# Gate rows of heads 1 to 3: from a product on TensorE to a broadcast load from DRAM

## The chip, the cores and the metric

The kernel runs on one core of a Trainium2 chip. The metric is the device time of one execution in microseconds (us), and the comparisons are between medians of several runs. A profile is one further execution, recorded by the hardware profiler. The engines are TensorE (PE in the rows; PEld is its weight load), VectorE (DVE), ScalarE (ACT), GpSimd (POOL) and SyncE (SP), which here only issues transfers.

## The reference

One encoder block works on 512 positions of 1024 channels. After an RMS norm, one projection makes the inputs of two branches. One branch is a Fourier mixing. The other is an mLSTM with 4 heads of 512 channels, run forward and backward. What matters here is the stabilised gate of the mLSTM. With `i` the input gate and `f` the log of the forget gate, per head and direction:

```python
bcum = jnp.cumsum(ft, axis=-1)
dmat = bcum[..., :, None] - bcum[..., None, :] + it[..., None, :]
m_t = jnp.maximum(bcum + m_st[..., None], jnp.max(dmat, axis=-1))
s_mat = jnp.einsum('bhtd,bhsd->bhts', qt, kt) * jnp.exp(dmat - m_t[..., None])
den = jnp.sum(s_mat, axis=-1) + inter * jnp.einsum('bhk,bhtk->bht', n_st, qt)
h_out = num / jnp.maximum(jnp.abs(den), jnp.exp(-m_t))[..., None]
```

The kernel computes the whole sequence at once instead of chunk by chunk. With `a = i - cumsum(f)` and `mx` the running maximum of `a` (starting at 0), the weight of source position s for target position t is `exp(a[s] - mx[t])`, and the stabiliser is `m = cumsum(f) + mx`. So each head and each direction needs two rows of 512 numbers in every partition: `mx` for the weights, and `m` for the lower bound `exp(-m)` of the denominator.

## The kernel before

The kernel is written with a tile framework. A planner orders each engine's instructions by simulated times, and it may move an instruction ahead of others that were written earlier. An instruction that is wrapped in `pin(...)` keeps its written order among the pinned ones. Tiles are taken by a tag. A new tile of the same tag takes the old one's place, and its first writer waits for the old one's last reader. PSUM is split into four banks of the tag `acc` and four of the tag `wk`.

The order of the work is: the projection of the mLSTM inputs and of a first gate (from the start to about 118 us), then four heads (to about 394 us, by the order of TensorE's products), then the mLSTM's output map, the Fourier branch and the merge. Products are made with float32 numbers split in two parts, a rounded part (ScalarE, `hi_of`, line 90) and the rest (VectorE, `lo_of`, line 93), and three products for one (`mm3`, lines 97 to 99).

Weights come in units of 128 x 1024 numbers. SyncE's queue loads a unit into one of three `raw` tiles (`fetch`, line 131; line 134 for halves), ScalarE and VectorE split it (`prepare`), and TensorE uses it. Each call of `unit()` splits one unit, hands out the one before it, and issues the fetch of the unit three further on. That fetch waits until VectorE has read the raw tile that it overwrites. The fetches are pinned. So are the copies of weight sums on SyncE's queue (line 159) and their accumulating counterparts on GpSimd's (line 163), which prepare sums for later stages (`sum_job`).

`gate_chain` (lines 420 to 457) runs once, in head 0. It makes, for all heads, a 64-row tile: row h is the forward direction of head h, row 32 + h the backward one. The last steps put the backward rows in natural order (lines 450 to 452). Then `mx` and `m` are split into a rounded part and a rest, in the tiles `mx_r` and `em_r` (lines 453 to 455), and `bsel`, a matrix of 8 selecting columns, is copied (line 456).

In each head:

- `decay` (line 512): for each direction TensorE multiplies a selecting column, repeated 128 times, with `mx_r` (line 516). That puts the head's row into all partitions of a PSUM bank. ScalarE makes the weights from it, eight exponentials (line 521) into the tiles `wf0` to `wf3`, and GpSimd cuts them at the diagonal (lines 525 and 528).
- The scores' products follow; VectorE multiplies them with the weights (lines 576 and 577) and sums them (lines 589 to 593).
- `o_unit` (lines 551 to 566, and 594 to 642) makes the output gate from four units. `o_gate` applies the sigmoid (line 572).
- The denominator: ScalarE writes a selecting tile `bw` (line 601), TensorE spreads the head's two rows of `em_r` with it (line 602, one product: the forward row in the upper 64 partitions and the backward row in the lower ones), and ScalarE takes `exp(-m)` (line 610). Line 608 sums the weighted scores. Line 612 takes their absolute value, line 613 the maximum of both, and line 614 the reciprocal.
- The weights are scaled and split (lines 622 to 628), values are made (line 636), the last output-gate unit follows (line 642), then the head's products, its norm (lines 652 to 658) and the transposes (line 668). Heads 1 to 3 also make their SiLU gate here, with `z_unit`.

Of the kernel before, what the change touches and what calls it, by code (L numbers as in the profile page):

```python
# [8 lines left out]
F32 = mybir.dt.float32  # L9
F32R = mybir.dt.float32r  # L10
AF = mybir.ActivationFunctionType
# [3 lines left out]
S = 512  # L15
D = 1024
P = 128
NH = 4
# [22 lines left out]
def hybrid_block(ctx: ExitStack, tc, xT, xn, first, units, blocks, vecs, gates, gbias, consts, dft, fnw, out):  # L41
    nc = tc.nc
    te, ve, se, gp = nc.tensor, nc.vector, nc.scalar, nc.gpsimd
# [17 lines left out]
    dram = ctx.enter_context(tc.tile_pool(name="sums", bufs=1, space=bass.MemoryType.DRAM))  # L61
# [3 lines left out]
    def tl(tag, shape, dtype=F32, bufs=1, pool=None, shift=0):  # L65
        count[0] += 1
        if pool is None:
            pool = "wide" if tag[:2] in ("sa", "sb") else "gw" if tag in ("gwh", "gwl") else "low" if tag in LOW else "high" if tag in HIGH else "work"


        n = math.prod(shape[1:])
        t = pools[pool][1].tile([shape[0], -(-(n + shift) // 64) * 64], dtype, tag=tag, name=f"{tag}_{count[0]}", bufs=bufs)
        t = t[:, shift : shift + n]
        if len(shape) == 2:
            return t
        names = "abcd"[: len(shape) - 1]
        return t.rearrange(f"p ({' '.join(names)}) -> p {' '.join(names)}", **dict(zip(names, shape[1:])))

    def bank(tag, cols=512, rows=P):
        count[0] += 1  # L80
        return ps.tile([rows, cols], F32, tag=tag, name=f"{tag}_{count[0]}", bufs=4)

    def t2k(dtype=F32, cols=S):
        return tl("t2k", [P, cols], dtype, bufs=3)

    def pin(ins, on=True):
        return tc.keep_in_program_order(ins) if on else ins
# [82 lines left out]
    def unit():  # L170
        i = state["split"]
        if state["at"] < len(JOBS) and i >= JOBS[state["at"]]:
            state["at"] += 1
            next_job()
        while len(items) < (4 if "gw" in pools else 2) and state["split"] < nplan:
            prepare()
        return items.pop(0)
# [39 lines left out]
    for n in range(4):  # L217
# [6 lines left out]
        for i in range(NU0):  # L224
            src, dst = slice(256 * i, 256 * i + 256), slice(256 * n, 256 * n + 256)
# [130 lines left out]
    def proj(hooks={}, pinned=False):  # L356
        wh, wl = unit()
        acc = bank("acc")
        for k in range(8):
            if k in hooks:  # L360
                hooks[k]()
            ks = slice(k * P, (k + 1) * P)
            mm3(acc, wh[:, ks], wl[:, ks], hv(x_hi, k), hv(x_lo, k), k == 0, k == 7, pinned or any(at <= k for at in hooks))
        return acc
# [19 lines left out]
    for n, (kind, i) in enumerate([("z", 0)] + [("x", i) for i in XO]):  # L384
# [6 lines left out]
        acc = early[n] if n < NU0 else proj(hooks, n == NU0 + 1)  # L391
# [24 lines left out]
    em_r = tl("em_r", [P, S], F32R)  # L416
    mx_r = tl("mx_r", [P, S], F32R)
    bsel = tl("bsel", [P, 8], F32R)

    def gate_chain():  # L420

        gb = tl("gb", [64, 2])
        pin(nc.sync.dma_start(gb, gbias))
        graw = t2k()
        se.activation(graw, gate_ps, AF.Copy)
        spare = [tl(t, [64, 2, S]) for t in ("so0", "so1")]
        s0, s1, s2, s3 = spare[0][:, 0, :], spare[0][:, 1, :], spare[1][:, 0, :], spare[1][:, 1, :]
        s4, s5 = tl("wf2", [64, S]), tl("wf3", [64, S])
        ig, z, e, u, w = s0, s1, s2, s3, s4
        for j, t in enumerate((ig, z)):  # L430
            sp = bank("acc", rows=64)
            te.matmul(sp, ident_c[:, C_SEL + 64 * j : C_SEL + 64 * j + 64], graw, start=True, stop=True)
            se.activation(t[0:32, :], sp[0:32, :], AF.Identity, bias=gb[0:32, j : j + 1])
            se.activation(t[32:64, ::-1], sp[32:64, :], AF.Identity, bias=gb[32:64, j : j + 1])
        se.activation(e, z, AF.Abs)
        se.activation(e, e, AF.Exp, scale=-1.0)
        ve.tensor_scalar(out=u, in0=e, scalar1=1.0, scalar2=None, op0=ALU.add)
        ve.scalar_tensor_tensor(out=w, in0=u, scalar=-1.0, in1=e, op0=ALU.add, op1=ALU.subtract)
        se.activation(u, u, AF.Ln)
        ve.scalar_tensor_tensor(out=w, in0=z, scalar=0.0, in1=w, op0=ALU.min, op1=ALU.add)  # L440
        ve.tensor_tensor(out=w, in0=w, in1=u, op=ALU.subtract)
        fc = e
        ve.tensor_tensor_scan(out=fc, data0=ones[0:64, 0:1].to_broadcast([64, S]), data1=w, initial=0.0,
                              op0=ALU.mult, op1=ALU.add)
        a, mx = u, z
        ve.tensor_tensor(out=a, in0=ig, in1=fc, op=ALU.subtract)
        ve.tensor_tensor_scan(out=mx, data0=a, data1=a, initial=0.0, op0=ALU.max, op1=ALU.max)
        ve.tensor_tensor(out=fc, in0=fc, in1=mx, op=ALU.add)
        an, mxn, mn = s5, s0, s4
        for dst, srct in ((an, a), (mxn, mx), (mn, fc)):  # L450
            ve.tensor_copy(dst[0:32, :], srct[0:32, :])
            ve.tensor_copy(dst[32:64, ::-1], srct[32:64, :])
        for dst, srct in ((mx_r, mxn), (em_r, mn)):
            se.activation(dst[0:64, :], srct, AF.Copy)
            ve.tensor_tensor(out=dst[64:128, :], in0=srct, in1=dst[0:64, :].bitcast(F32), op=ALU.subtract)
        pin(se.activation(bsel, ident_c[:, C_BSEL : C_BSEL + 8], AF.Copy))
        return an

    def gate_cols(an):
# [14 lines left out]
    for h in range(NH):  # L474
# [21 lines left out]
        for d in range(4):  # L496
            acc = bank("wk")
# [7 lines left out]
        if h == 0:  # L505
            rows = gate_chain()
# [5 lines left out]
        def decay():  # L512
            ws = [tl(f"wf{b}", [P, 640]) for b in range(4)]
            for dr in range(2):
                bc = bank("acc")
                te.matmul(bc, bsel[:, 4 * dr + h : 4 * dr + h + 1].to_broadcast([P, P]), mx_r, start=True, stop=True)
                for b in range(4):
                    n = (b + 1) * P
                    o, s = (slice(n, 640), slice(b * P, S)) if dr == 0 else (slice(0, n), slice(0, n))
                    r = 32 * dr + h  # L520
                    se.activation(ws[b][:, o], bc[:, s], AF.Exp, scale=-1.0, bias=a_col[:, b, r : r + 1])
            for b in range(4):
                n = (b + 1) * P
                blk = ws[b][:, n : n + P]
                gp.affine_select(out=blk, in_=blk, compare_op=ALU.is_ge, fill=0.0, base=0,
                                 pattern=[[1, P]], channel_multiplier=-1)
                blk = ws[b][:, n - P : n]
                gp.affine_select(out=blk, in_=blk, compare_op=ALU.is_ge, fill=0.0, base=0,
                                 pattern=[[-1, P]], channel_multiplier=1)
            return ws  # L530
# [20 lines left out]
        def o_part(n, w, pieces):  # L551
            wh, wl = w
            for k2, t in pieces:
                k = 2 * n + k2
                ts = slice(t * P, (t + 1) * P)
                ks = slice(k2 * S, (k2 + 1) * S)
                te.matmul(ops[t], hv(x_hi, k)[:, ts], wh[:, ks], start=k == 0, stop=False)  # L557
                te.matmul(ops[t], hv(x_hi, k)[:, ts], wl[:, ks], start=False, stop=False)  # L558
                te.matmul(ops[t], hv(x_lo, k)[:, ts], wh[:, ks], start=False, stop=k == 7)  # L559
# [3 lines left out]
        def o_unit(n):  # L563
            o_part(n, unit(), PIECES)
# [5 lines left out]
        def o_gate():  # L570
            for t in range(4):
                se.activation(so[t], ops[t], AF.Sigmoid, scale=rc[:, t : t + 1])
# [22 lines left out]
        early = 3 if h == 0 else 0  # L595
        w2 = unit()
        o_part(2, w2, PIECES[:early])
        em, bc, den = tl("phi2", [P, S]), bank("wk"), bank("wk")
        halves = [slice(0, 64), slice(64, 128)]
        bw = tl("plo2", [P, 2, 64], F32R)  # L600
        se.activation(bw, bsel.bitcast(F32).rearrange("p (r i) -> p r i", r=2)[:, :, h : h + 1].to_broadcast([P, 2, 64]), AF.Copy)
        te.matmul(bc, bw.rearrange("p r m -> p (r m)"), em_r, start=True, stop=True)
        for dr, acc in enumerate((sf, sb_)):
            sh, sl = tl(f"vhi{3 - dr}", [P, S], F32R), tl(f"vlo{3 - dr}", [P, S], F32R)
            hi_of(sh, acc)
# [1 line left out]
            for part, rr in enumerate((sh, sl)):  # L607
                te.matmul(den, half_r[:, dr, :], rr,  # L608
                          start=dr == 0 and part == 0, stop=dr == 1 and part == 1)
        se.activation(em, bc, AF.Exp, scale=-1.0)  # L610
        r = t2k()
# [20 lines left out]
        for b in range(4):  # L632
# [7 lines left out]
            vh.append(a_)  # L640
            vl.append(b_)
        o_unit(3)
        o_gate()
        if h > 0:
            z_unit(0)
        ss = tl("ss", [P, 4], bufs=2)
        for t in range(4):
# [7 lines left out]
            r = tl("rr", [P, 1], bufs=4)  # L655
# [47 lines left out]
    for q in range(2):  # L703
        accs = [bank("acc") for _ in range(4)]
        for n in range(8):
# [6 lines left out]
            for k in range(8):  # L712
                j, c = (n, k) if n < 4 else (2 * (n % 2) + k // 4, 4 * (n // 2) + k % 4)
# [214 lines left out]
    for j in range(8):  # L928
        ga = gates_a[j]
        wh, wl = unit()  # L930
        acc = bank("acc")
# [35 lines left out]
    rows = {}  # L967
# [192 lines left out]
```

## Time and profile before

| what | value |
|---|---|
| median of 3 runs | 755.77 us (755.54 to 756.1) |
| the profiled execution | 755.68 us |
| its span, first to last instruction | 753.9 us |
| mean granted clock of TensorE | 0.999 |
| busy: TensorE, VectorE, ScalarE, GpSimd | 743.9, 527.5, 410.9, 68.9 us |
| instructions of line 516 and line 602 | 8 and 4 |

Rows of the profile name a source line of the kernel as L516. A row in the order of time has the start (us from the span's beginning), the length, the engine, the line, the operation, the tile written and the tiles read, the shapes and a count; idle time of the engine just before it and what ended it stand in brackets. A row of a wait says who waited for whom: us in total, how often, and the longest. A row of a group has busy time and the mean length of one. A row of one line's instructions has shortest, median and longest in ns. Matmul ends are modelled, and a product overlaps the next one, so what one product costs is the distance to the next start.

### The profile page before, as it was taken

How to read it: one execution, taken by the hardware profiler on the slowest of the kernel's cores; microseconds unless marked ns; L12 is line 12 of the kernel's file. 1: busy time of each engine (PE TensorE's matmuls, PEld its weight loads, DVE VectorE, ACT ScalarE, POOL GpSimd, SP SyncE). 2: the span in 40 equal slices, each digit the busy share in tenths (PEclk: the TensorE clock that was granted, in tenths of full speed). 3: DMA queues.
4: the chain of work that ended last, by engine and by line, in shares of the span. 5: the costliest groups of instructions: out<-in, count | busy, mean ns of one | idle time of the engine just before them, and what ended most of it. 6: DMA issues, size and time to landing. Idle time of an engine off the chain costs nothing.

```text
span 753.9 us, 10931 instructions
## 1 busy us (share of the span) xinstructions
PE 743.9 (99%) x4140; PEld 641.5 (85%) x4140; DVE 527.5 (70%) x830; ACT 410.9 (55%) x645; POOL 68.9 (9%) x143
## 2 busy tenths in 40 slices
PE   8999999999999999999999999999999999999996
PEld 7888875888888888888888888899999999988885
DVE  6999983696759475767584757257667787566976
ACT  7345466468447752776263343265544587543444
POOL 0001000104100310041002110000010100000003
PEclk9999999999999999999999999999999999999999
DMA  8538865176924892479314964366655456554452
GB/s 291 179 140 230 232 232 144 39 235 160 214 109 156 213 229 75 168 180 228 122 51 152 222 201 148 93 199 205 201 165 152 146 168 197 168 184 157 135 196 111
DMA packets 40947, 128.62 MB, mean 171 GB/s; under 512 B 4800, under 2 KB 5568, under 8 KB 35776
## 3 DMA queue, kind: packets, MB, share of 16 engines
q1 hardware_dynamic: 36944, 104.47, 40.8%
q0 software_dynamic: 3520, 23.07, 15.3%
q8 instruction: 32, 0.52, 0.3%
q10 hardware_dynamic: 432, 0.40, 0.2%
q14 instruction: 19, 0.16, 0.1%
HBM read 125.82 MB, written 44.04 MB: 225 GB/s over the span
## 4 chain that ended last, share of the span: by engine, by line
PE 96%; DVE 1%; ACT 1%; DMA 1%; POOL 0%; issue 0%; POOLq 0%; ACTq 0%
PE acc L97 17%; PE acc L98 17%; PE acc L99 17%; PE wk L97 8%; PE wk L98 8%; PE wk L99 8%; PE acc L557 3%; PE acc L559 3%; PE acc L558 3%; PE wk L636 2%; PE acc L1010 1%; PE acc L1009 1%; PE acc L1008 1%; PE wk L668 1%; PE wk L302 1%; PE wk L608 1%
## 5 line engine op out<-in xcount | busy, mean ns | idle before, releaser
L93 DVE TENSOR_TENSOR wlo<-raw,whi 128x1024 fp32r<-128x1024 f32 (+2 forms) x107 | 124.9, 1172 | 80.0 <-ACT whi L90 79.8
L90 ACT ACTIVATE whi<-raw 128x1024 fp32r<-128x1024 f32 (+2 forms) x107 | 108.6, 1020 | 128.9 <-PE acc L98 76.1
L97 PE MATMUL acc<-hhi,whi 128*128 128x512 f32 x240 | 94.3, 393 | 1.2 <-ACT whi L90 1.2
L98 PE MATMUL acc<-hlo,whi 128*128 128x512 f32 x240 | 93.5, 390 | 0.0
L99 PE MATMUL acc<-hhi,wlo 128*128 128x512 f32 x240 | 93.5, 390 | 0.0
L93 DVE TENSOR_TENSOR gwl<-raw,gwh 128x1024 fp32r<-128x1024 f32 (+1 forms) x39 | 47.1, 1208 | 16.3 <-ACT gwh L90 16.2
L90 ACT ACTIVATE gwh<-raw 128x1024 fp32r<-128x1024 f32 (+1 forms) x39 | 40.8, 1047 | 26.6 <-PE acc L98 7.8
L97 PEld LDWEIGHTS acc<-hhi,whi 128*128 128x128 f32 x240 | 45.1, 188 | 11.8 <-ACT whi L90 1.8
L99 PEld LDWEIGHTS acc<-hhi,wlo 128*128 128x128 f32 x240 | 45.1, 188 | 9.5
L98 PEld LDWEIGHTS acc<-hlo,whi 128*128 128x128 f32 x240 | 45.1, 188 | 9.0
L559 PE MATMUL acc<-whi,hlo 128*128 128x512 f32 x128 | 50.4, 394 | 0.0
L558 PE MATMUL acc<-wlo,hhi 128*128 128x512 f32 x128 | 50.3, 393 | 0.0
L98 PE MATMUL acc<-sb,whi 128*128 128x512 f32 x128 | 50.1, 391 | 0.0
L97 PE MATMUL acc<-sa,whi 128*128 128x512 f32 x128 | 49.8, 389 | 0.0
L98 PE MATMUL wk<-vlo,phi 128*128 128x512 f32 x128 | 49.8, 389 | 0.0
L97 PE MATMUL wk<-vhi,phi 128*128 128x512 f32 x128 | 49.6, 389 | 0.0
L99 PE MATMUL acc<-sa,wlo 128*128 128x512 f32 x128 | 49.0, 391 | 0.0
L99 PE MATMUL wk<-vhi,plo 128*128 128x512 f32 x128 | 48.0, 389 | 0.0
L557 PE MATMUL acc<-whi,hhi 128*128 128x512 f32 x128 | 47.7, 393 | 0.0
L331 DVE SCALAR_TENSOR_TENSOR t2k<-sa,vecs,t2k 128x511 f32<-128x511 f32 (+1 forms) x64 | 45.1, 744 | 0.1
L93 DVE TENSOR_TENSOR vlo<-wk,vhi 128x512 fp32r<-128x512 f32 x32 | 20.5, 676 | 15.7 <-ACT vhi L90 15.7
L98 PEld LDWEIGHTS wk<-vlo,phi 128*128 128x128 f32 x128 | 24.0, 188 | 5.0
(409 smaller groups left out, 1908.8 us busy)
## 6 DMA issues: line engine op xcount, KB each, us to landing
raw<-in_units_dram SPq DMA_DIRECT2D x69, 512.0 KB, 4.0
sum<-in_blocks_dram SPq DMA_DIRECT2D x20, 1024.0 KB, 8.2
raw<-sum SPq DMA_DIRECT2D x64, 256.0 KB, 3.8
raw<-in_blocks_dram SPq DMA_DIRECT2D x48, 256.0 KB, 3.9
sum<-in_blocks_dram POOLq DMA_DIRECT2D x10, 1024.0 KB, 9.2
sum<-sum POOLq DMA_DIRECT2D x10, 1024.0 KB, 8.4
raw<-sum SPq DMA_DIRECT2D x8, 512.0 KB, 4.4
raw<-in_blocks_dram SPq DMA_DIRECT2D x6, 512.0 KB, 4.0
```

Of the source, the lines that this page charges most:

```text
L90: pin(se.activation(dst, src, AF.Copy, scale=scale), pinned)
L93: pin(ve.tensor_tensor(out=dst, in0=src, in1=hi.bitcast(F32), op=ALU.subtract), pinned)
L97: pin(te.matmul(acc, wh, xh, start=start, stop=False, **skip), pinned)
L98: te.matmul(acc, wh, xl, start=False, stop=False, **skip)
L99: te.matmul(acc, wl, xh, start=False, stop=stop, **skip)
L302: pin(te.matmul(gate_ps[rows, :], w_gate[j][:, i, :], r, start=n == 0, stop=n == 14, tile_position=(0, 32 * (2 * b + j))), n + b + j > 0)
L331: ve.scalar_tensor_tensor(out=cv[:, o], in0=src[:, s], scalar=cw[k], in1=cv[:, o], op0=ALU.mult, op1=ALU.add)
L557: te.matmul(ops[t], hv(x_hi, k)[:, ts], wh[:, ks], start=k == 0, stop=False)
L558: te.matmul(ops[t], hv(x_hi, k)[:, ts], wl[:, ks], start=False, stop=False)
L559: te.matmul(ops[t], hv(x_lo, k)[:, ts], wh[:, ks], start=False, stop=k == 7)
L608: te.matmul(den, half_r[:, dr, :], rr, start=dr == 0 and part == 0, stop=dr == 1 and part == 1)
L636: te.matmul(vp[:, ds], xm[c0 + d][:, b * P : (b + 1) * P], vbf[:, d, :], start=True, stop=True)
```

## The change

After the gate chain, the 64 rows of `mx` and of `m` are also stored to two DRAM tensors, by two transfers that GpSimd issues. A new function `spread_rows(h)` issues four loads on SyncE's queue. Two put the rows of `mx` of head h, forward and backward, into all 128 partitions of a tile each. They take the tags `mx_r` and `em_r`. Two put the rows of `m` into the upper and lower 64 partitions of a tile with the new tag `em`, of which there is one buffer. The function is called in heads 0 to 2 for the next head, after that head's last output-gate unit, and its loads are pinned.

Heads 1 to 3 take the exponentials of `decay` from these tiles. They compute `exp(-m)` in place in `em`, and no longer issue the products of lines 516 and 602 or the copy of line 601. Head 0 computes as before. The reversed `m` now lies in a tile with the tag `em` instead of `wf2`.

```diff
--- before.py
+++ after.py
@@ -417,6 +417,19 @@
     mx_r = tl("mx_r", [P, S], F32R)
     bsel = tl("bsel", [P, 8], F32R)
 
+    kept_rows = [dram.tile([64, S], F32, tag=f"rows{j}", name=f"rows{j}") for j in range(2)]
+    spread = {}
+
+    def spread_rows(h):
+        for dr in range(2):
+            r = 32 * dr + h
+            spread[dr] = tl(("mx_r", "em_r")[dr], [P, S])
+            pin(nc.sync.dma_start(spread[dr], kept_rows[0][r : r + 1, :].to_broadcast([P, S])))
+        spread[2] = tl("em", [P, S])
+        for dr in range(2):
+            r = 32 * dr + h
+            pin(nc.sync.dma_start(spread[2][64 * dr : 64 * dr + 64], kept_rows[1][r : r + 1, :].to_broadcast([64, S])))
+
     def gate_chain():
 
         gb = tl("gb", [64, 2])
@@ -446,7 +459,7 @@
         ve.tensor_tensor(out=a, in0=ig, in1=fc, op=ALU.subtract)
         ve.tensor_tensor_scan(out=mx, data0=a, data1=a, initial=0.0, op0=ALU.max, op1=ALU.max)
         ve.tensor_tensor(out=fc, in0=fc, in1=mx, op=ALU.add)
-        an, mxn, mn = s5, s0, s4
+        an, mxn, mn = s5, s0, tl("em", [P, S])[0:64]
         for dst, srct in ((an, a), (mxn, mx), (mn, fc)):
             ve.tensor_copy(dst[0:32, :], srct[0:32, :])
             ve.tensor_copy(dst[32:64, ::-1], srct[32:64, :])
@@ -454,6 +467,8 @@
             se.activation(dst[0:64, :], srct, AF.Copy)
             ve.tensor_tensor(out=dst[64:128, :], in0=srct, in1=dst[0:64, :].bitcast(F32), op=ALU.subtract)
         pin(se.activation(bsel, ident_c[:, C_BSEL : C_BSEL + 8], AF.Copy))
+        for dst, srct in zip(kept_rows, (mxn, mn)):
+            nc.gpsimd.dma_start(dst, srct)
         return an
 
     def gate_cols(an):
@@ -512,8 +527,11 @@
         def decay():
             ws = [tl(f"wf{b}", [P, 640]) for b in range(4)]
             for dr in range(2):
-                bc = bank("acc")
-                te.matmul(bc, bsel[:, 4 * dr + h : 4 * dr + h + 1].to_broadcast([P, P]), mx_r, start=True, stop=True)
+                if h > 0:
+                    bc = spread[dr]
+                else:
+                    bc = bank("acc")
+                    te.matmul(bc, bsel[:, 4 * dr : 4 * dr + 1].to_broadcast([P, P]), mx_r, start=True, stop=True)
                 for b in range(4):
                     n = (b + 1) * P
                     o, s = (slice(n, 640), slice(b * P, S)) if dr == 0 else (slice(0, n), slice(0, n))
@@ -595,11 +613,15 @@
         early = 3 if h == 0 else 0
         w2 = unit()
         o_part(2, w2, PIECES[:early])
-        em, bc, den = tl("phi2", [P, S]), bank("wk"), bank("wk")
+        if h > 0:
+            em, bc, den = spread[2], spread[2], bank("wk")
+        else:
+            em, bc, den = tl("phi2", [P, S]), bank("wk"), bank("wk")
         halves = [slice(0, 64), slice(64, 128)]
-        bw = tl("plo2", [P, 2, 64], F32R)
-        se.activation(bw, bsel.bitcast(F32).rearrange("p (r i) -> p r i", r=2)[:, :, h : h + 1].to_broadcast([P, 2, 64]), AF.Copy)
-        te.matmul(bc, bw.rearrange("p r m -> p (r m)"), em_r, start=True, stop=True)
+        if h == 0:
+            bw = tl("plo2", [P, 2, 64], F32R)
+            se.activation(bw, bsel.bitcast(F32).rearrange("p (r i) -> p r i", r=2)[:, :, 0:1].to_broadcast([P, 2, 64]), AF.Copy)
+            te.matmul(bc, bw.rearrange("p r m -> p (r m)"), em_r, start=True, stop=True)
         for dr, acc in enumerate((sf, sb_)):
             sh, sl = tl(f"vhi{3 - dr}", [P, S], F32R), tl(f"vlo{3 - dr}", [P, S], F32R)
             hi_of(sh, acc)
@@ -640,6 +662,8 @@
             vh.append(a_)
             vl.append(b_)
         o_unit(3)
+        if h < NH - 1:
+            spread_rows(h + 1)
         o_gate()
         if h > 0:
             z_unit(0)
```

## The prediction

> **What bounds the kernel now.** I read the page first, for the engine that fills the span and for the chain that ends last:
>
> ```profile
> PE 743.9 (99%) x4140; PEld 641.5 (85%) x4140; DVE 527.5 (70%) x830; ACT 410.9 (55%) x645; POOL 68.9 (9%) x143
> PE 96%; DVE 1%; ACT 1%; DMA 1%; POOL 0%; issue 0%; POOLq 0%; ACTq 0%
> ```
>
> TensorE is busy for 99% of the span, and 96% of the last chain is its work. Busy time is modelled, so I looked next at what TensorE waited for in the whole span, and at the start times of neighbouring products (here around the row product of line 602 in head 2):
>
> ```profile
> PE acc L97 <- ACT whi L90: 1.2, 1, 1.2
> PE wk L196 <- POOL mhalf L183: 1.1, 1, 1.1
> PE wk L608 <- ACT vhi L90: 0.5, 1, 0.5
> ...
> 298.91 0.39 PE L99 MATMUL acc<-hhi,wlo 128*128 128x512 f32 x1
> 299.14 0.39 PE L97 MATMUL acc<-hhi,whi 128*128 128x512 f32 x1
> 299.36 0.39 PE L602 MATMUL wk<-em_r,plo 128*128 128x512 f32 x1
> 299.59 0.39 PE L98 MATMUL acc<-hlo,whi 128*128 128x512 f32 x1
> 299.82 0.39 PE L99 MATMUL acc<-hhi,wlo 128*128 128x512 f32 x1
> ```
>
> Three waits, 2.8 us in all. A 512-column product lasts 0.39 us, but the next starts after a quarter of a microsecond: four steps from 298.91 to 299.82 are 0.91 us, so one costs 0.227 us of the stream. The stream of products is the bound: an edit pays what it takes out of the stream, and costs what it adds in waits.
>
> **What is removed.** Heads 1 to 3 lose two products at line 516 and one at line 602 each: nine of 512 columns. Their rows in the order of time show what each takes from the stream:
>
> ```profile
> 169.18 0.40 PE L516 MATMUL acc<-mx_r,bsel 128*128 128x512 f32 x1
> 169.42 0.39 PE L97 MATMUL wk<-vhi,phi 128*128 128x512 f32 x1
> 169.65 0.40 PE L98 MATMUL wk<-vlo,phi 128*128 128x512 f32 x1
> 170.05 0.49 PE L516 MATMUL acc<-mx_r,bsel 128*128 128x512 f32 x1
> 170.39 0.40 PE L97 MATMUL wk<-vhi,phi 128*128 128x512 f32 x1
> ...
> 238.69 0.63 PE L516 MATMUL acc<-mx_r,bsel 128*128 128x512 f32 x2
> 239.16 0.39 PE L99 MATMUL acc<-hhi,wlo 128*128 128x512 f32 x1
> ...
> 313.88 0.63 PE L516 MATMUL acc<-mx_r,bsel 128*128 128x512 f32 x2
> 314.35 0.39 PE L99 MATMUL acc<-hhi,wlo 128*128 128x512 f32 x1
> ```
>
> - Head 1: the first takes 169.42 - 169.18 = 0.24. From 169.65 to 170.39 there are 0.74, of which the product at 169.65 itself needs 0.23; the other 0.51 go with the second one, its short wait for a bank included (it writes a PSUM bank that the output gate's sigmoid had to leave first).
> - Heads 2 and 3: 239.16 - 238.69 = 0.47 and 314.35 - 313.88 = 0.47.
> - Line 602: 299.59 - 299.36 = 0.23, three times 0.23 = 0.69 (the three are alike: one group, minimum 388 and maximum 389 ns).
>
> Sum: 0.24 + 0.51 + 0.47 + 0.47 + 0.69 = 2.38 us.
>
> [...]
>
> Line 601 goes three times, and with it the idle time of ScalarE in front of it:
>
> ```profile
> L601 ACT ACTIVATE plo<-bsel x4: 309/309/309, 137.8 to 372.4; 128x128 fp32r<-128x128 f32 x4
>   PE wk L99: 25.6, 3
> ```
>
> ScalarE stood 25.6 us in front of these three copies until the scores' products let go of the tile, and no TensorE wait points at it. I cost this, the two freed accumulator banks, the freed bank of line 602 and the exponentials that now read SBUF at nothing: TensorE's own stream covers them. If that cover were gone, they would be gains (0.31 us a copy), not losses.
>
> **What is added in head 0.** Two stores of 64 rows by GpSimd. Their sources are ready when VectorE ends its last two reversing copies, and GpSimd has nothing to do then:
>
> ```profile
> 135.75 0.42 DVE L452 COPY so<-so 32x512 f32<-32x512 f32 x1
> 136.63 0.42 DVE L452 COPY wf<-so 32x512 f32<-32x512 f32 x1
> 122.50 0.84 POOL L163 DMA_DIRECT2D sum<-sum  x1
> 144.98 0.29 POOL L525 TENSOR_SCALAR_AFFINE_SELECT wf<-wf 128x128 f32<-128x128 f32 x1 [21.64 <-ACT wf L521]
> ```
>
> One issue costs 0.84 on GpSimd. Two, from 137.05 (136.63 + 0.42), end at 138.7, over 6 us ahead of the selects of head 0 that are queued behind at 144.98: nothing. Should the planner put them among the selects, whose results VectorE awaits, the bound is 2 x 0.84 = 1.7 us. The stabilisers move from a tile of the weights (wf2) to a new one, which only frees the old one sooner.
>
> **What is moved, and the new wait.** Four loads per head (two of 256 KB, two of 128 KB) go onto SyncE's queue, in written order, behind the raw weight tile fetched in the last output-gate unit (`o_unit(3)`). That call splits one unit and fetches the one three further on. Counting units through the splits, its fetches are those at 167.12, 200.68 and 275.89; so these are the queue's neighbours, with VectorE's line 613 and the splits (ScalarE, line 90) that need the fetches behind:
>
> ```profile
> 167.12 0.34 SPq L131 DMA_DIRECT2D raw<-in_units_dram  x1
> 167.50 0.49 SPq L159 DMA_DIRECT2D sum<-in_blocks_dram  x1
> ...
> 200.68 0.33 SPq L131 DMA_DIRECT2D raw<-in_units_dram  x1
> 211.08 0.33 SPq L131 DMA_DIRECT2D raw<-in_units_dram  x1
> 275.89 0.33 SPq L131 DMA_DIRECT2D raw<-in_units_dram  x1
> 284.74 0.33 SPq L131 DMA_DIRECT2D raw<-in_units_dram  x1
> ...
> 226.35 0.69 DVE L613 TENSOR_TENSOR t2k<-t2k,phi 128x512 f32<-128x512 f32 x1 [1.26 <-ACT t2k L612]
> 305.40 0.69 DVE L613 TENSOR_TENSOR t2k<-t2k,phi 128x512 f32<-128x512 f32 x1
> ...
> 238.26 1.06 ACT L90 ACTIVATE whi<-raw 128x1024 fp32r<-128x1024 f32 x1 [2.75 <-PE acc L98]
> 315.11 1.05 ACT L90 ACTIVATE whi<-raw 128x1024 fp32r<-128x1024 f32 x1
> ...
> DMA to landing us min/median/max: 3.2/4.7/11.6
> ```
>
> The last line is the landing of the raw fetches from 172 to 330 us; I use it for the broadcast loads, which the trace does not show: 3.2 at best, 11.6 at worst, 4.7 taken, since they have the size of half a raw tile or less.
>
> - Head 1's rows: nothing holds them (the tiles were last read in head 0). Issued at 167.5, 167.8, 168.1 and 168.5; the copy at 167.50 slips by 1.3 us. They land at about 172 to 173.
> - Head 2's rows: the two maxima's rows go out at about 201. The stabilisers' tile (`em`) is single, and its last reader is line 613 of head 1. So SyncE stands from about 201.7 until 226.35 + 0.69 = 227.04, 25 us, and the raw fetch of 211.08 stands behind it. It leaves at 227.0 + 3 x 0.33, about 227.8, after the two halves of `em`. The split three further on starts at 238.26: 10.5 us for a landing.
> - Head 3's rows: the same, from about 277 to 306.09; the fetch of 284.74 leaves at about 306.8, and its split starts at 315.11: 8.3 us for a landing.
>
> At 4.7 us both fit with over 3 us to spare, so the new wait costs nothing; at 11.6 the first is 1.1 and the second 3.3 us late, 4.4 together. The rows themselves have time in heads 2 and 3. In head 1 they meet the exponentials, which ran early:
>
> ```profile
> 174.67 1.78 ACT L521 ACTIVATE wf<-acc,a_col 128x512 f32<-128x512 f32 x4
> 179.10 0.68 ACT L654 ACTIVATE t2k<-so 128x512 f32<-128x512 f32 x1
> 183.49 0.63 ACT L654 ACTIVATE t2k<-so 128x512 f32<-128x512 f32 x1 [0.22 <-DVE so L652]
> 211.20 0.29 DVE L576 TENSOR_TENSOR wf<-wk,wf 128x128 f32<-128x128 f32 x1 [0.15 <-PE wk L99]
> ```
>
> The first reader of their result is at 211.20, over 30 us later, so they could slide; at 172 they need not.
>
> **The sum.** The profiled execution took 755.68 us for a span of 753.9. 755.68 - 2.38 = 753.30. The median of the runs is 0.09 above the profiled one: **753.4 us**, 0.31% less. About 0.2% (1.5 us) can be told from no change: faster is below 754.26, slower above 757.28.
>
> **The rivals.**
>
> 1. *The planner's new order gives part of it back.* Whatever is not pinned is laid out anew, and the trace shows the size of one miss: 1.2 us at line 97 and 0.47 at line 608. One miss of 1.2 leaves 754.6; a miss together with the 1.7 us of GpSimd in head 0 leaves 756.3. For it: ScalarE and VectorE are 55% and 70% busy and their order shifts once line 601 is gone. Against it: TensorE has one wait, of 0.5 us, in all four heads.
> 2. *Head 1's rows land late.* If the exponentials keep their place and the rows land more than 174.67 - 167.5 = 7.2 us after issue, ScalarE stands, and the squares at 179.10 to 183.49 with it, which feed the head's transposes. At 10.6 us the hold is 3.4 and, with no cover taken, the time 756.8. Against it: 30 us in which the planner can move them.
> 3. *Slower: SyncE's hold starves the splits.* The place is the `em` load in front of the raw fetches in heads 1 and 2. Beyond a landing of 10.5 us in the one and 8.3 in the other each microsecond is lost to the split, and, with no cover taken, to TensorE. The gain is used up when (x - 10.5) + (x - 8.3) = 2.38, at x = 10.6 us; slower by 0.2% begins at 11.4; at 15 us it is 4.5 + 6.7 - 2.4 = 8.8, or 764.6. For it: landings up to 11.6 are in the trace, and 128 reads of one 2 KB row are not. Against it: those long landings fell beside 1 MB copies, and behind the hold the queue's next copies come after 237 and 312 us. [...]
> 4. *More than the nine.* If the 0.47 at line 608 goes as well: 752.9.
>
> That the nine products stay is excluded: the code no longer issues them.
>
> **How the numbers follow.** Forecast 0.54 (own range 753.0 to 754.2), rival 1 0.15, rival 2 0.10, rival 3 0.15, rival 4 0.06. Faster is the forecast and rival 4, 0.60; same is rivals 1 and 2, 0.25; slower is rival 3, 0.15. The range reaches from 752.3 (rival 4 with another half microsecond) to 757.8 (the start of rival 3): below it I leave some 0.05, above it 0.12.
>
> **What would show it.** Right: TensorE with nine products fewer, its waits no longer than 3 us, neighbours at 0.227 us where the rows stood; SyncE waiting some 25 to 30 us for line 613 in heads 1 and 2 with the splits at 238 and 315 not waiting for a DMA. Wrong: a ScalarE wait for a raw tile in these heads (rival 3), exponentials of head 1 that wait for a load (rival 2), a new TensorE wait elsewhere (rival 1), or a broadcast load that takes over 10 us.

## The result and the profile after

The changed kernel takes **780.1 us** (median of 4 runs, 778.79 to 783.01) against 755.65 us before (4 runs, 755.49 to 756.1): a ratio of 1.0327, interval 1.0314 to 1.0339. It is 24.5 us slower; the prediction was 753.4 us, with a range of 752.3 to 757.8. The profiled execution took 779.45 us for a span of 777.5. Lines 516, 525, 602 and 613 of before are now lines 534, 543, 624 and 635; the row loads are at 427 (maxima) and 431 (stabilisers), the stores at 471.

The page's busy times and its chain that ended last:

```profile
PE 751.7 (97%) x4131; PEld 645.3 (83%) x4131; DVE 528.2 (68%) x830; ACT 411.1 (53%) x642; POOL 69.7 (9%) x145
PE 92%; DMA 3%; ACT 2%; DVE 1%; issue 1%; SPq 1%; POOL 0%; POOLq 0%; ACTq 0%
```

The waits of TensorE and of SyncE's queue (total us, times, longest):

```profile
PE acc L97 <- ACT whi L90: 12.0, 3, 7.5
PE wk L97 <- ACT phi L90: 3.6, 1, 3.6
PE acc L575 <- ACT whi L90: 1.7, 1, 1.7
...
SPq L431 <- DVE t2k L635: 72.2, 2, 36.3
```

TensorE has its nine products fewer (4131 for 4140), yet is busy 7.8 us longer, and its longest waits are now for splits by ScalarE (line 90). SyncE stands twice in front of the load into `em`, 72.2 us together, for line 635. To see where TensorE stood, its own rows around the stalls, in the order of time:

```profile
168.09 0.39 PE L577 MATMUL acc<-whi,hlo 128*128 128x512 f32 x1
172.12 0.79 PE L97 MATMUL wk<-vhi,phi 128*128 128x512 f32 x1 [3.64 <-ACT phi L90]
...
174.71 0.63 PE L576 MATMUL acc<-wlo,hhi 128*128 128x512 f32 x1
175.13 0.63 PE L577 MATMUL acc<-whi,hlo 128*128 128x512 f32 x1
...
243.58 0.40 PE L99 MATMUL acc<-hhi,wlo 128*128 128x512 f32 x1
251.53 0.80 PE L97 MATMUL acc<-hhi,whi 128*128 128x512 f32 x1 [7.54 <-ACT whi L90]
...
327.98 0.39 PE L99 MATMUL acc<-hhi,wlo 128*128 128x512 f32 x1
332.34 0.80 PE L97 MATMUL acc<-hhi,whi 128*128 128x512 f32 x1 [3.97 <-ACT whi L90]
332.93 0.63 PE L98 MATMUL acc<-hlo,whi 128*128 128x512 f32 x1
335.23 0.80 PE L575 MATMUL acc<-whi,hhi 128*128 128x512 f32 x1 [1.67 <-ACT whi L90]
```

Beyond the usual step of 0.23 us the four stalls are 3.80, 7.72, 4.13 and 2.07 us, 17.7 together. They are not the whole loss: after each long stall the products go on at half pace. The two rows at 174.71 and 175.13 are 0.42 us apart, where 0.227 was the step. The view by stretches (length, busy times with instruction counts, then the granted clock, the DMA share and GB/s) puts that on the clock:

```profile
160.00:168.00 8.00, 8.00 (x45) 6.93 (x44) 1.98 (x3) 2.07 (x4) 0.00 (x0) 1.00 0.96 314
172.12:177.50 5.38, 5.38 (x12) 3.86 (x13) 4.44 (x9) 5.37 (x8) 0.00 (x0) 0.52 0.73 270
180.00:190.00 10.00, 10.00 (x46) 8.27 (x45) 3.89 (x8) 7.16 (x17) 5.21 (x14) 1.00 0.56 131
251.53:255.70 4.17, 4.17 (x10) 3.06 (x11) 4.17 (x8) 3.54 (x6) 0.00 (x0) 0.50 0.47 155
...
332.34:341.30 8.96, 7.29 (x17) 5.27 (x18) 7.48 (x14) 8.86 (x13) 1.02 (x4) 0.51 0.65 235
```

In the three stretches behind the long stalls the granted clock is 0.52, 0.50 and 0.51. Their 12, 10 and 17 products would need 2.7, 2.3 and 3.9 us at 0.227; over that, and over the 2.07 us of stall inside the last one, the stretches lost 2.7, 1.9 and 3.0, together 7.6 us. So 17.7 of stalls and 7.6 of half clock, less the 2.4 of the removed products: 22.9 of the 23.6 us by which the span grew (777.5 for 753.9).

**The hold of SyncE's queue.** The queue's issues in head 1, before and after. Before:

```profile
196.74 0.33 SPq L131 DMA_DIRECT2D raw<-in_units_dram  x1
197.11 0.50 SPq L159 DMA_DIRECT2D sum<-in_blocks_dram  x1
200.68 10.73 SPq L131 DMA_DIRECT2D raw<-in_units_dram  x2
```

After:

```profile
202.28 0.33 SPq L131 DMA_DIRECT2D raw<-in_units_dram  x1
202.66 0.43 SPq L427 DMA_DIRECT2D mx_r<-rows  x1
203.14 0.42 SPq L427 DMA_DIRECT2D em_r<-rows  x1
239.92 1.12 SPq L431 DMA_DIRECT2D em<-rows  x2
241.09 0.59 SPq L159 DMA_DIRECT2D sum<-in_blocks_dram  x1
241.78 1.77 SPq L131 DMA_DIRECT2D raw<-in_units_dram  x3
```

The loads stand between the raw fetch of 196.74 and the sum copy, so the fetch of 200.68 is behind them too, not ahead. Three raw fetches leave together at 241.78, after a hold from 203.6 to 239.9. The first landed at 248.3; ScalarE's split of it came at 250.43, and TensorE, whose last product had started at 243.58, went on at 251.53. Head 2 repeats it: `em` at 322.70, the fetches from 324.56, the first of them landed at 331.2, its split at 331.23, TensorE at 332.34. In this kernel ScalarE is no earlier than the landing: from 243.73 to 250.43 it works without a pause on line 632 and what stands behind it, so 2.1 us of the stall in head 1 are its order, and in head 2 it comes free just as the fetch lands. That the fetch alone holds the split is seen in `e2_exp_in_its_head` below.

**The hold of ScalarE.** ScalarE's rows in front of the first stall, in head 0, and of the second:

```profile
165.89 0.63 ACT L632 ACTIVATE em<-em 128x512 f32<-128x512 f32 x1 [8.59 <-DMA em<-rows]
166.43 1.26 ACT L640 ACTIVATE phi<-t2k 64x512 f32<-64x512 f32 x2
...
171.33 0.74 ACT L90 ACTIVATE phi<-wf 128x640 fp32r<-128x640 f32 x1 [0.28 <-DVE wf L647]
...
243.73 1.28 ACT L632 ACT_TABLE_LOAD   x1 [2.27 <-DMA em<-rows]
245.02 0.63 ACT L632 ACTIVATE em<-em 128x512 f32<-128x512 f32 x1
...
250.43 1.99 ACT L90 ACTIVATE whi<-raw 128x1024 fp32r<-128x1024 f32 x2
```

Line 632 is `exp(-m)`. At 165.89 it is that of head 1, but it stands among the copies of head 0. It needs only the loaded rows, no longer a product of its own head, and the planner put it a head early. ScalarE runs its list in order, so it stood 8.59 us for the load, and the copies of line 640, which head 0's weights need, stood behind. The split that TensorE then waited for came at 171.33. In heads 1 and 2 the same line waits 2.27 and 2.05 us for the loads that SyncE had held.

### The profile page after: what moved, and what is told of

Read it like the earlier page. It is cut to its first block, busy times and chain, and to the rows that moved or that the text cites. A ratio compares the mean times of both kernels' runs of the same rounds, so it can differ in the third digit from the quotient of the medians.

```text
span 777.5 us, 10933 instructions
## 1 busy us (share of the span) xinstructions
PE 751.7 (97%) x4131; PEld 645.3 (83%) x4131; DVE 528.2 (68%) x830; ACT 411.1 (53%) x642; POOL 69.7 (9%) x145
## 4 chain that ended last, share of the span: by engine, by line
PE 92%; DMA 3%; ACT 2%; DVE 1%; issue 1%; SPq 1%; POOL 0%; POOLq 0%; ACTq 0%
PE acc L97 17%; PE acc L98 17%; PE acc L99 17%; PE wk L97 7%; PE wk L98 7%; PE wk L99 7%; PE acc L575 4%; PE acc L576 3%; PE acc L577 3%; DMA em<-rows 1%; PE acc L1032 1%; PE acc L1034 1%; PE acc L1033 1%; PE wk L302 1%; PE wk L692 1%; DMA raw<-in_units_dram 1%
## 5 line engine op out<-in xcount | busy, mean ns | idle before, releaser
L97 PE MATMUL acc<-hhi,whi 128*128 128x512 f32 x240 | 96.0, 400 | 12.0 <-ACT whi L90 12.0
L98 PE MATMUL acc<-hlo,whi 128*128 128x512 f32 x240 | 95.3, 397 | 0.0
L97 PEld LDWEIGHTS acc<-hhi,whi 128*128 128x128 f32 x240 | 46.2, 193 | 23.8 <-ACT whi L90 13.6
L97 PEld LDWEIGHTS wk<-vhi,phi 128*128 128x128 f32 x128 | 24.4, 191 | 9.1 <-ACT phi L90 4.1
L575 PEld LDWEIGHTS acc<-whi,hhi 128*128 128x128 f32 x128 | 24.7, 196 | 8.3 <-ACT whi L90 2.8
```

What stands on the lines that cost most here:

```text
L97: pin(te.matmul(acc, wh, xh, start=start, stop=False, **skip), pinned)
L98: te.matmul(acc, wh, xl, start=False, stop=False, **skip)
```

## The experiments

Two theories were set against each other. Ratios are against `before` in the same group of runs, 755.47 to 755.55 us. **H**: the loss is two holds of engines that work in order, SyncE's (one buffer of `em`, raw fetches behind it; 36.3 us at the longest) and ScalarE's (an exponential that can be placed a head early; 8.59 us). **T**: it is the transfers themselves, or the new order of everything else.

### One hold taken away at a time

`e1_two_em_tiles` gives `em` two buffers, so that SyncE needs to wait for nobody:

```diff
-        spread[2] = tl("em", [P, S])
+        spread[2] = tl("em", [P, S], bufs=2)
...
-        an, mxn, mn = s5, s0, tl("em", [P, S])[0:64]
+        an, mxn, mn = s5, s0, tl("em", [P, S], bufs=2)[0:64]
```

> The tag em gets two buffers, so the load of the next head's stabilisers no longer waits for line 635 of the head. Theory H (SyncE's hold in front of the raw fetches makes the stalls in heads 1 and 2): their stalls of 7.7, 4.1 and 2.1 us and the products at half pace behind them (2.3 and 3.1 us) go, 19.3 us in all: 780.1 - 19.3 = 760.8 us; the stall at the end of head 0 (3.8 us and 2.7 us at half pace) stays. Rival T (the added transfers themselves starve the raw tiles, or the planner's new order of the gate's products does): the time stays above 772 us.

Measured: 778.13 us (777.42 to 780.47), ratio 1.0303 (1.0285 to 1.0321). The expectation missed by 17 us. SyncE's wait for line 635 is gone, but ScalarE's rows among the waits are now these:

```profile
ACT em L632 <- DMA em<-rows: 13.4, 2, 9.3
ACT L632 <- DMA em<-rows: 8.7, 1, 8.7
```

Now all three exponentials stand a head early, and ScalarE stood 22.1 us in front of them. TensorE stalled at 167.9 (4.5 us), 219.6 (4.6) and 291.5 (4.2). One hold removed fed the other.

`e2_exp_in_its_head` leaves the single buffer and keeps the exponential, and the two splits of the scores' sums ahead of it, in written order:

```diff
-            hi_of(sh, acc)
+            hi_of(sh, acc, pinned=h > 0)
...
-        se.activation(em, bc, AF.Exp, scale=-1.0)
+        pin(se.activation(em, bc, AF.Exp, scale=-1.0), h > 0)
```

> The exponential of em (line 632) is pinned behind the splits of the scores' sums of its own head, so ScalarE no longer meets it a head early; em keeps its one buffer. Theory H: ScalarE's 8.6 us in front of it in head 0 go, and with them TensorE's stall of 3.8 us at 168 us and the half pace behind it, 2.7 us: 780.1 - 6.5 = 773.6 us; the stalls of heads 1 and 2 stay. Rival (the stall at 168 us comes from the raw tiles or from the output gate's sigmoids): within 1.5 us of 780.1.

Measured: 769.05 us (768.73 to 769.75), ratio 1.0178 (1.0161 to 1.0195), 4.5 us less than expected. ScalarE no longer waits for `em`, and the stall in head 0 is gone. SyncE's hold stays among the waits, and TensorE's for the splits:

```profile
PE acc L97 <- ACT whi L90: 10.1, 3, 5.1
...
SPq L431 <- DVE t2k L635: 71.6, 2, 36.0
```

In the order of time, TensorE around the first of its two long stalls, and ScalarE's split that it waited for:

```profile
236.94 0.40 PE L99 MATMUL acc<-hhi,wlo 128*128 128x512 f32 x1
242.47 0.80 PE L97 MATMUL acc<-hhi,whi 128*128 128x512 f32 x1 [5.13 <-ACT whi L90]
...
241.36 1.06 ACT L90 ACTIVATE whi<-raw 128x1024 fp32r<-128x1024 f32 x1 [1.45 <-DMA raw<-in_units_dram]
```

Here ScalarE stands for the raw tile itself, 1.45 us in head 1 and 2.59 in head 2: this is SyncE's hold starving the splits, with nothing of ScalarE's own in front.

So keeping the exponential in its head gives back 11 of the 24.5 us, more than head 0's 6.5: in heads 1 and 2 the exponential no longer stands in front of the splits either, and the stalls there are 11.5 us together for 13.9. SyncE's hold, with its half clock, stays: 13.6 us over `before` in the same group.

### Both taken away

`e5_two_tiles_exp_in_head` has both edits above. `e6_late_load_exp_in_head` keeps one buffer and the pinned exponential, and issues the loads of `em` at the head's end, behind the next four raw fetches:

```diff
+    def spread_em(h):
         spread[2] = tl("em", [P, S])
...
+        if h < NH - 1:
+            spread_em(h + 1)
```

> Both repairs together: two buffers for em, and line 632 pinned in its own head. Theory H (the loss is the two holds, SyncE's before line 635 and ScalarE's before an exponential whose rows have not landed): no wait for a row load is left, so 755.5 - 2.4 = 753.1 us, up to 757 if the loads cost the later stage what the run with the maxima alone lost there (3.5 us of waits after 420 us). Rival T (the transfers starve the raw tiles): above 760 us, with ScalarE waiting for raw tiles in heads 1 and 2.

> One em buffer; the two stabiliser loads of a head move to the end of the head ahead, behind its last raw fetches, where line 635 is long done; line 632 pinned in its own head. Theory H: neither hold, the same as with two buffers, 753 to 757 us. If the single buffer itself or the early place of the loads matters otherwise: above 760 us.

Measured: e5 757.4 us (9 runs, 756.39 to 760.91), ratio 1.0028 (1.0017 to 1.0039); e6 757.24 us (11 runs), 1.0025 (1.0017 to 1.0034). In both, no exponential stands for `em`. SyncE's hold is gone in e5; in e6 it is 7.6 us in two waits, behind the four raw fetches. So line 635 was not long done there, against the expectation, but TensorE's waits are as short as in e5. With the holds, by different means, 22.7 us are gone: that settles H for the bulk of the loss. The two costs do not add: ScalarE's hold alone is worth 20.7 us (e1 against e5), SyncE's alone 11.7 (e2 against e5), both together 22.7.

But the kernels are still 1.9 and 1.7 us slower than before, just past the 757 us that the expectations allowed. TensorE's longest waits in e5:

```profile
PE acc L97 <- ACT whi L90: 1.7, 3, 0.9
...
PE acc L99 <- DVE wlo L93: 1.1, 2, 0.5
```

And two stretches, ahead of 420 us and behind it, of before:

```profile
0.00:420.00 420.00, 417.23 (x1965) 341.58 (x1966) 302.04 (x475) 240.27 (x373) 50.76 (x103) 1.00 0.59 172
420.00:455.00 35.00, 35.00 (x158) 28.97 (x157) 26.15 (x42) 15.69 (x22) 3.12 (x5) 1.00 0.76 219
```

and of e5:

```profile
0.00:420.00 420.00, 417.63 (x1967) 341.88 (x1967) 300.12 (x472) 239.56 (x370) 47.37 (x102) 1.00 0.59 175
420.00:455.00 35.00, 33.11 (x144) 25.99 (x143) 27.47 (x42) 15.06 (x23) 5.63 (x8) 1.00 0.95 251
```

At 420 us e5 has issued 1967 products for 1965, and has nine fewer to issue: it is 11 ahead, 2.5 us, the forecast gain. In the next 35 us it issues 144 for 158, 14 fewer, 3.2 us. The gain comes out of the heads as predicted and is lost, with more, behind them, where both clocks are 1.00. That is the profiled run of e5, 0.6 us longer in its span than before's; the median of e5's runs lies another 1.0 us above it.

### The transfers alone

`e7_transfers_alone` is the kernel before with the two stores and the twelve loads, into tiles that nothing reads:

```diff
+            t = tl(("ea", "eb")[dr], [P, S])
+            pin(nc.sync.dma_start(t, kept_rows[0][r : r + 1, :].to_broadcast([P, S])))
...
+        for dst, srct in zip(kept_rows, (mxn, mn)):
+            nc.gpsimd.dma_start(dst, srct)
```

> The kernel before, all its products kept, plus the two stores and the four loads per head at the same place, into three tiles that nobody reads; no load waits for a compute engine. The output is the reference's. Theory H: within 2 us of the kernel before, 755.5 to 757.5 us. Rival T (traffic is the loss): 765 us or more.

Measured: 755.34 us (11 runs, 755.19 to 755.82), ratio 0.9999 (0.999 to 1.0007). Its loads of `em` took, from issue to landing:

```profile
DMA to landing us min/median/max: 6.2/14.1/14.3
```

14 us, three times what the prediction took, and no cost: T falls for the transfers. With e5, whose loads took up to 16.2 us and whose longest wait of TensorE was 1.1 us, it also shows that slow loads cost nothing in these heads, where no engine stood for them.

### The two halves of the change

`e3_maxima_only` loads the maxima only; lines 601 and 602 stay, and there is no `em` tile to be held. `e8_maxima_loaded_earlier` is the same with the loads two output-gate units earlier. `e4_stabilisers_only` loads `m` only, with the single buffer and the free exponential, and keeps the products of line 516. `e10_stabilisers_repaired` is e4 with both repairs.

```diff
e3:
-            spread[dr] = tl(("mx_r", "em_r")[dr], [P, S])
+            spread[dr] = tl(("mx_r", "em")[dr], [P, S])
-        spread[2] = tl("em", [P, S])
...
e4:
-        for dr in range(2):
-            r = 32 * dr + h
-            spread[dr] = tl(("mx_r", "em_r")[dr], [P, S])
...
+                bc = bank("acc")
+                te.matmul(bc, bsel[:, 4 * dr + h : 4 * dr + h + 1].to_broadcast([P, P]), mx_r, start=True, stop=True)
```

> Heads 1 to 3 load only the rows of the maxima; the stabilisers keep line 601 and the product of line 602. No load waits for a late reader. Theory H: no hold, no early exponential; the six products are saved: 755.65 - 1.69 = 754.0 us. Rival T (traffic or the order that the planner makes once the two accumulator banks are free): above 757 us, with waits for raw tiles.

> The maxima alone, as before, but the two loads are issued after the head's second output-gate unit instead of after its fourth. Theory H: the heads have no new wait either way, so -1.69 us there; what the later stage adds depends on the planner's order and can be anything from 0 to 4 us: 753.8 to 758. If the place of the loads is what costs: the time changes by more than 3 us against 758.6.

> Heads 1 to 3 load only the rows of the stabilisers (one buffer); the maxima keep the two products of line 516. Theory H: the whole loss is the em tile's, so it stays: 780.1 + 1.7 = 781.8 us, within 6 us as the planner's order shifts. Rival T (the loads of the maxima or the freed accumulator banks make it): below 762 us.

> The stabilisers alone by loads, with both repairs; the maxima keep their six products. Theory H: no hold, so the 766.0 us of the same kernel without repairs fall to 755.5 - 0.69 = 754.8 us; theory L agrees, since the accumulator banks are used as before. Rival (any shift of the heads costs the later stage its 3 us): 757 us or more.

Measured: e3 758.64 us, 1.0041 (1.0025 to 1.0057); e8 758.92, 1.0048 (1.0036 to 1.006); e4 766.04, 1.0138 (1.0122 to 1.0153); e10 756.16, 1.0008 (0.9999 to 1.0016).

e3 has no hold at all, as expected, but it missed its time by 4.6 us: its waits lie behind 420 us, where it issues 145 products in the 35 us. e8's are the same, with its loads landed in 4 to 6.7 us, so where the maxima are loaded is not the cause; it lies 0.9 us above its expected range. e4 shows both holds without the maxima:

```profile
SPq L427 <- DVE t2k L628: 64.6, 2, 34.7
...
ACT em L625 <- DMA em<-rows: 6.3, 1, 6.3
ACT L625 <- DMA em<-rows: 5.8, 2, 3.5
```

It lost 10.6 us where 26 were expected: the holds are nearly as long, but TensorE stalled once for long (5.0 us at 316.23), where the full change stalls in three places. In head 1 the hold ended at 229.75 and TensorE had products until 242, with a wait of 0.5 us; in the changed kernel it ended at 239.92 and the products ran out at 243.8. A hold's length does not give its price; how many prepared products are left when it ends does. With both repairs (e10) all but 0.6 us of it is gone. e10 missed its 754.8 by 1.4 us: the gain of its three products is not seen. By the count at 420 us, e3 and e10 are level with before (1959 and 1962 products, six and three fewer to issue), not ahead.

### The late waits

Behind 420 us lies the output map, which the change does not touch. A theory **L** put its new waits down to what head 3 frees. `e9_head3_keeps_products` is e5 with head 3's maxima by the products of line 516; `e11_head3_maxima_alone` loads the maxima for head 3 alone, and no `m`.

```diff
e9:
-                if h > 0:
+                if h in (1, 2):
e11:
-        for dr in range(2):
+        for dr in range(2 if h in (3,) else 0):
```

> Both repairs (two em tiles, line 632 pinned in its head), but head 3 keeps its two products for the maxima; heads 1 and 2 load theirs. Theory L (the waits after 420 us, some 3 us in the runs without any hold, come from the order that the planner makes once head 3's products and their two accumulator banks are gone): they go, and 755.5 - 2.38 + 0.47 = 753.6 us. Rival (they come from any shift of the heads): 756.5 to 758 us.

> Only head 3's maxima come by loads; all other products stay. Theory L: two products less, 0.47 us, and the late waits appear: 755.5 - 0.47 + 3 to 3.5 = 758 to 758.5 us. Rival (the late waits come from the shift that heads 1 and 2 bring): 755.0 us.

Measured: e9 756.41 us (11 runs), 1.001 (1.0001 to 1.0018); e11 755.81 (12 runs), 1.0003 (0.9994 to 1.0012). Both are nearer to the rival's times than to L's. In e9 most of the late waits are gone, but a new one stands in the heads (1.0 us at line 575, for VectorE). In e11 they hardly appear (0.4 and 0.2 us at lines 97 and 99): L falls as a single cause, since head 3's part alone does not bring them.

One thing goes with them in every run without long stalls. GpSimd's accumulating copy of this stage, queued behind head 3's norms, of before:

```profile
414.31 0.93 POOL L163 DMA_DIRECT2D sum<-sum  x1
```

and of e5:

```profile
420.65 0.93 POOL L163 DMA_DIRECT2D sum<-sum  x1
```

It starts between 420.6 and 421.8 in e3, e5, e6 and e8, which have the late waits, and between 414.3 and 416.7 in before, e7, e9, e10 and e11, which do not or hardly. The norms ahead of it moved with it: head 3's products were laid out later there, although TensorE's stream was ahead. The DMA share of the 35 us is 0.92 to 0.95 in the first group and 0.76 to 0.86 in the second. Whether the late copy, the late norms or the splits queued beside them make TensorE wait was not told apart; holding head 3's order as it was would need that order written out, and was not tried.

## Why the prediction was wrong

1. *TensorE's stream is the bound, and nine products are worth 2.38 us*: right where all nine go and no hold is left. e5 and e6 are 11 and 10 products ahead at 420 us. With fewer removed (e3, e10) the gain was not seen there.
2. *The stores cost nothing*: right. GpSimd's rows in the order of time show the second store and the first select, which started at 144.98 before:

```profile
137.38 0.54 POOL L471 DMA_DIRECT2D rows<-em  x1 [0.18 <-issue]
145.02 0.29 POOL L543 TENSOR_SCALAR_AFFINE_SELECT wf<-wf 128x128 f32<-128x128 f32 x1 [7.10 <-ACT wf L539]
```

   e7 bears it out.
3. *The loads stand behind the raw tile fetched in the last output-gate unit, which fetches the unit three further on*: **the step that failed first**. The call that splits a unit fetches the one two further on (three from the one that it hands out). Its fetch in head 1 is that of 196.74, not of 200.68; in heads 0 and 2 it is likewise the one before. So not one fetch stood behind the hold but three, and the first of them was the next unit that the splits needed. The 10.5 us of room belonged to the second.
4. *SyncE stands from 201.7 to 227.04*: the wait and its end at line 613 are right, the length is not. It took 36.3 us, until 239.92. The end was read from before, as if nothing ahead of it could move; it moved by 12.9 us. Some 6.5 of that are head 0's new stall (3.80, and 2.7 at half clock). In e2, without that stall, the hold still ended 5.8 us later than forecast, at 232.82: the planner had put more of head 1's other products ahead of those that line 635 awaits. Line 630, the sum that it needs, starts at 229.91 behind 1059 products, where before it was 224.15 behind 1032.
5. *The price of a hold is the landing time beyond the room* (rival 3, whose place was right): the form holds, the room was mis-sized. In head 1 the first fetch left at 241.78. TensorE's products ran out at 243.81, and it went on 1.1 us after the split's start, so the split was due at 242.7: 0.9 us of room, not 10.5. The landing of 6.5 us, well inside the 3.2 to 11.6 of the prediction, was 5.6 too long; the other 2.1 of the 7.72 us are ScalarE's order. Slow row loads, which the rival feared, were not the cause: e5 and e7 had loads of 14 to 16 us and no wait of TensorE over 1.1 us.
6. *The exponentials that now read SBUF cost nothing*: **the second failed step**. Rival 2 looked at the decay exponentials, which ran at 179.9 without a wait. The one that held ScalarE was `exp(-m)`: the change took away the product that had kept it in its head. It cost 11 us beside SyncE's hold (e2 against the changed kernel) and 20.7 without it (e1 against e5).
7. *A microsecond of wait costs a microsecond*: too little. The 17.7 us of stalls took 7.6 us of half clock with them.
8. *Rival 1, the new order gives part of it back*: right in kind, as e5 and e6 show, though off in place (behind 420 us) and in size (4 us, more than the whole gain).

The chances had 0.15 on the right rival and put its price at 764.6 us for a landing of 15 us. Counting the queue's neighbours right would have shown a loss without any slow transfer. Of the two fetches that share the row at 200.68 in before, the first is the unit that ScalarE splits at 233.53, and that of 275.89 the unit that it splits at 307.04, in the same profile of before:

```profile
233.53 1.06 ACT L90 ACTIVATE whi<-raw 128x1024 fp32r<-128x1024 f32 x1
...
307.04 1.06 ACT L90 ACTIVATE whi<-raw 128x1024 fp32r<-128x1024 f32 x1 [0.33 <-PE acc L98]
```

Behind holds until 227.04 and 306.09, the two `em` loads and the sum copy (1.9 us in the changed kernel), these fetches leave at about 229 and 308. With the prediction's own 4.7 us they land at about 233.6 and 312.6: on time in head 1, and 5.6 us late in head 2, more than the whole gain. The later end of the holds, ScalarE's hold and the half clock came on top.

Two sums of the prediction are off by 0.1 to 0.2 us (three issues from 227.0 end at 228.0, not 227.8; 752.9 less half a microsecond is 752.4, not 752.3). Nothing hung on them.

## What to carry to other kernels

Before a load is put on a queue that also prefetches, name the last reader of its buffer and the first prefetch behind it: if the reader comes later than that prefetch is needed, the queue starves its engine, as it did here with loads of `m` that landed in 2.8 to 6.3 us but stood up to 36.3 us in front of the fetches. When a dependency is removed, ask what it had been holding in place: an instruction that becomes ready early may be laid out early, and an engine that works in order then stands in front of it, as ScalarE did for 8.59 us in head 0. And where a dense stream of products is the bound, weigh what is taken out of it against one stall: here 2.4 us against the 3.80 us of head 0, which brought 2.7 us of half clock with them.

## What the runs showed of the hardware

**The clock after a stall.** In the changed kernel the products behind the stalls of 3.80, 7.72 and 4.13 us were mostly 0.43 us apart, for 5.2, 4.1 and 8.6 us (the last with a second stall, of 2.07 us, inside). The granted clock in these stretches was 0.50 to 0.52, and 1.00 between them. In e1 and e2 the rows at 224.50 and 242.47, behind waits of 4.48 and 5.13 us, lasted 0.79 and 0.80 us, as the first rows behind those three stalls did, for 0.39 where the clock was 1.00. Behind a wait of 1.31 us in e4 (the row at 169.50) the steps were 0.33, 0.24 and 0.23 us, and the longest wait of e3, 1.5 us, lies in 35 us with a granted clock of 1.00. How long a stall has to be to bring the half clock was not shown.

**Loads of one row into 128 partitions.** 256 KB that way landed in 4.4 to 15.4 us in the changed kernel, and the 128 KB of `m` in 2.8 to 6.3; in e7 the latter had a median of 14.1. The prediction's 4.7 was no bound, but nothing hung on it.
